# The second 1024 columns of the gates and projections computed with tokens stationary

## The chip, the cores and the metric

The kernel runs on one core of a Trainium2 chip. The metric is the device time of one execution in microseconds, the median of several runs.

## The reference

One decoder block over 256 tokens of width 2048, all in fp32. From the condition vector `c` six vectors of 2048 are made with the matrix `w_ada` (they scale, shift and gate). Then:

```
proj = h @ w_in                       # h: normed, scaled, shifted x
u, q, k, v, ga, gb = split(proj)      # 1024, 1024, 1024, 1024, 2048, 2048 columns
y_ssm = s5_branch(u)                  # state-space scan, gelu, times sigmoid(y @ w_glu + b)
y_att = moba_attention(q, k, v)
merged = sigmoid(ga) * (y_ssm @ w_proj_ssm) + sigmoid(gb) * (y_att @ w_proj_attn)
x = x + g1 * (merged @ w_out)
x = x + g2 * (square(relu(h2 @ w_ff1)) @ w_ff2)
return rms_norm(x, g)
```

## The kernel before

**Matmuls in three pieces.** Each fp32 operand is split in two fp32r parts, a rounded `hi` and the rest `lo`, and a product is hi*hi + hi*lo + lo*hi. For weights this is done as they stream in (`stream`, `split`): SP issues a load of 128 rows by 1024 columns, 512 KB, into one of 7 `wraw` buffers (L153), ScalarE casts `whi` (L158), VectorE subtracts to `wlo` (L160), each in 4 buffers. Such a k tile of 1024 columns is called a unit here.

**Two forms of a pass.** A pass takes one group of 1024 weight columns through all its k tiles, into four PSUM banks of a ring of five. `gemm_t` (L194 to L196) keeps the weights stationary and streams the 256 tokens: 8 blocks of 128 columns, three matmuls of 256 columns each, 24 a unit; the result lies with weight columns on the partitions and tokens along the row. `gemm_n` (L235 to L237) keeps 128 tokens stationary and streams 512 weight columns: 2 token halves, 2 column halves, three matmuls each, 12 a unit; the result has tokens on the partitions. `w_out` and `w_ff2` and the values of attention use `gemm_n`; q, k, u, the gates and the projections use `gemm_t`.

**The order of work around the change.** After q, k, v, u and the first half of `ga` come three passes over `w_in` of 16 units each: the second half of `ga` (5120), `gb` first half (6144) and second half (7168). Then, of 8 units each: proj_attn columns 0 to 1023, w_glu, proj_attn columns 1024 to 2047, proj_ssm in two passes; then w_out in two passes of 16 units. The attention runs between the matmuls of the first gate pass, the scan from its ninth unit on through the other two.

**Lanes.** Side jobs sit in lanes. After each unit `step` adds the lane's rate to its credit and starts a job for each whole credit. The lane `ada` holds the sums for `w_ada`: a job loads 512 KB into a `wraw` buffer (L289) and has VectorE multiply and sum an earlier one (L296). Its rate is set by stage: R4 for the last 12 units of k and v, RS0 for the first 8 units of the second `ga` pass, RS1 from there, RS2 in the last gate pass, RS3 in proj_attn 0, RPA from w_glu to proj_ssm, RWO in w_out. The lane `m` holds attention at rate RAT, then 14 scan jobs at rate RSS: for each of four blocks the inputs, the scan and the outputs, then gelu and `hop_out`, which turns the result around by 32 small DMAs on POOL's queue into `yT`. Within this, the order on each engine is fixed at build time by the framework's scheduler, from priorities and its own estimate of times.

**From the scan to the merge.** `yT` holds tokens as (s c), s being the position within four. It is split into `yy` (`split` called with `sc4`), the input of w_glu; its sigmoid `sg` is multiplied by `yT` (L1201) and split into `gg`, the input of proj_ssm. All these keep the (s c) order of tokens. `gb` is multiplied by the proj_attn banks (L1181). The merge then, bank by bank, multiplies `ga` by the proj_ssm bank and restores the order of tokens on the way by a view with stride four on `ga` (L1212), adds `gb` (L1213) and splits the sum into `mh`, `ml`, the stationary operands of w_out.

Of the kernel before, what the change touches and what calls it, by code (L numbers as in the profile page):

```python
# [19 lines left out]
P = 128  # L20
S = 256
D = 2048
KT = D // P
# [24 lines left out]
R1 = .92  # L48
R2 = .56
R3 = .0  # L50
R4 = .5
RS0 = .6
RS1 = .3
RS2 = .3
RS3 = .7
GR = (4, 6, 6)
RAT = 1.5
RSS = .43
RPA = .88
RWO = .6  # L60
RM = 1.05
# [15 lines left out]
class Kern:  # L77
# [136 lines left out]
                                               stop=i == n - 1 and k == 1, skip_group_check=True)  # L214
        return banks

    def gemm_n(self, src, kts, c0, xh, xl, koff=0, tail=1):
        nc = self.nc
        banks = self.four("pn")
        n = len(kts)  # L220
        held, prev = [], None
        for i, unit in enumerate(self.stream(src, kts, c0)):
            u = (i,) + unit
            held.append(u)
            for t in range(2):
                if t and n - tail <= i < n - 1:
                    continue
                tk = slice(t * P, (t + 1) * P)
                for s in range(2):
                    o = banks[t * 2 + s]  # L230
                    c = slice(s * 512, (s + 1) * 512)
                    for q, kt, hi, lo in held if t else [u]:
                        kx = kt - koff
                        with self.after(prev if tail > 1 and i == n - 1 and t + s else None):
                            nc.tensor.matmul(o, xh[:, kx, tk], hi[:, c], start=q == 0, stop=False)  # L235
                            nc.tensor.matmul(o, xl[:, kx, tk], hi[:, c], start=False, stop=False)  # L236
                            self.mm = last = nc.tensor.matmul(o, xh[:, kx, tk], lo[:, c], start=False, stop=q == n - 1)  # L237
                    prev = last
                if t:
                    held = []  # L240
        return banks
# [658 lines left out]
    def body(self):  # L900
        nc, a, v = self.nc, self.a, self.nc.vector
# [62 lines left out]
        win = a["w_in"][0]  # L964
# [130 lines left out]
        nop = lambda: None  # L1095
# [26 lines left out]
        self.flush("ssm")  # L1122
        self.lanes["ada"][1] = R4
        self.bias_load()
        qkvu(1, 2, 2)
        qkvu(2, 2, 2)
        ga = self.ga
        self.asc = ga[:, 8:14, :].rearrange("p k s -> p (k s)").rearrange("p (i n) -> p i n", i=2)
        self.yatt = self.slot("S5", [P, 8, S], name="yatt")
        gb = self.slot("S1", [P, KT, S], name="gb")  # L1130
        tabs = {}

        def start():
# [14 lines left out]
        self.lane("m", self.attn_jobs() + [start], RAT, 1.0)  # L1148
        self.lanes["ada"][1] = RS0

        def to_ssm():
            self.flush("m")
            self.lane("m", bgl, RSS)
            self.lanes["ada"][1] = RS1

        for i in range(1, 4):
            if i == 3:
                self.lanes["ada"][1] = RS2
            dst, c0 = ((ga, 4096), (ga, 5120), (gb, 6144), (gb, 7168))[i]
            banks = self.gemm_t(win, range(KT), c0, self.ah, self.al, mid={8: to_ssm} if i == 1 else {})  # L1160
            for b in range(4):
                nc.scalar.copy(dst[:, (i % 2) * 8 + 2 * b:(i % 2) * 8 + 2 * b + 2, :],
                               banks[b].rearrange("p (k s) -> p k s", s=S))
        self.flush("m")
        self.lanes["ada"][1] = RS3

# [6 lines left out]
        yh = self.slot("SV", [P, 8, S], F32R, name="yh")  # L1173
        yl = self.slot("T", [P, 8, S], F32R, name="yl")
        for k in range(4):
            self.split(yh[:, 2 * k:2 * k + 2], yl[:, 2 * k:2 * k + 2], self.yatt[:, 2 * k:2 * k + 2])
        def proj_attn(cg):
            banks = self.gemm_t(a["w_proj_attn"][0], range(8), cg * 1024, yh, yl)
            for b in range(4):
                d = gb[:, cg * 8 + 2 * b:cg * 8 + 2 * b + 2, :].rearrange("p k s -> p (k s)")  # L1180
                v.tensor_mul(d, d, banks[b])  # L1181

        proj_attn(0)
        self.lanes["ada"][1] = RPA
        yy = self.slot("VT", [P, 2, 8, S], F32R, name="yy")
        yT = self.yT.rearrange("p s k c -> p k s c")
        sc4 = lambda z: z.rearrange("p k (s c) -> p k s c", s=4)
        self.gate, self.hgate = self.done[-4]
        for k in range(4):
            self.split(sc4(yy[:, 0, 2 * k:2 * k + 2]), sc4(yy[:, 1, 2 * k:2 * k + 2]), yT[:, 2 * k:2 * k + 2])  # L1190
# [1 line left out]
        banks = self.gemm_t(a["w_glu"][0], range(8), 0, yy[:, 0], yy[:, 1])  # L1192
        gg = self.slot("QT", [P, 2, 8, S], F32R, name="gg")
        sg = self.slot("S5", [P, 4, 2, S], name="sg")
        for b in range(4):
            t = sg[:, b]
# [3 lines left out]
            s = slice(2 * b, 2 * b + 2)  # L1200
            v.tensor_mul(sc4(t), sc4(t), yT[:, s])  # L1201
            self.split(gg[:, 0, s], gg[:, 1, s], t)
        proj_attn(1)
        m2 = self.slot("A2", [P, 2, KT, S], F32R, name="mh")
        mh, ml = m2[:, 0], m2[:, 1]
        for cg in range(2):
            banks = self.gemm_t(a["w_proj_ssm"][0], range(8), cg * 1024, gg[:, 0], gg[:, 1])
            for b in range(4):
                s = slice(cg * 8 + 2 * b, cg * 8 + 2 * b + 2)
                d = ga[:, s, :]  # L1210
                dk = d.rearrange("p k (c s) -> p k s c", s=4)
                v.tensor_mul(dk, dk, banks[b].rearrange("p (k s c) -> p k s c", k=2, s=4))  # L1212
                v.tensor_add(d, d, gb[:, s, :])  # L1213
                self.split(mh[:, s], ml[:, s], d)
        self.lane("x", self.load_x(), .25, -.5)
        self.lane("g1", [lambda ch=ch: g1_row(ch) for ch in range(4)], .25)
        self.lanes["ada"][1] = RWO
# [3 lines left out]
        for cg in range(2):  # L1221
# [6 lines left out]
            banks = self.gemm_n(a["w_out"][0], range(KT), cg * 1024, mh, ml, tail=TW if cg else 1)  # L1228
# [3 lines left out]
            with self.hot():  # L1232
                for b in range(4):
                    t, c = b // 2, slice(cg * 1024 + (b % 2) * 512, cg * 1024 + (b % 2) * 512 + 512)
# [141 lines left out]
        for g in range(NP):  # L1376
            part = self.slot(("S4", "T", "SV", "S5")[g], [P, 4, 512], name="part")
            if g:
                banks = self.gemm_t(w1, range(0, 8), g * 1024, self.ah, self.al)
            else:  # L1380
                wh, wl = [self.slot(n, [P, 4, 1024], F32R, name="wf") for n in ("VT", "QT")]
                banks = self.gemm_t(w1, range(0, 4), 0, hp[:, 0], hp[:, 1], mid={2: h_first, 3: h_second},
                                    homes=[(wh[:, k, :], wl[:, k, :]) for k in range(4)])
# [79 lines left out]
```

## Time and profile before

| | |
|---|---|
| median of 3 runs | 1403.18 us (1402.85 to 1406.64) |
| the profiled execution | 1404.23 us, of which the span is 1402.5 us |
| TensorE matmul busy | 1374.0 us, 9704 matmuls |
| VectorE busy | 1062.9 us |
| ScalarE busy | 702.7 us |
| DMA | 356.61 MB, 254 GB/s over the span |

PE is TensorE, PEld its weight loads, DVE VectorE, ACT ScalarE, SP the engine that issues the weights' DMAs, POOL GpSimd. A group's row names the line, the engine, the operation, what is written and read, the shapes, the count, busy microseconds and mean nanoseconds of one, and after a bar the idle time just before them with what ended it. A windows row gives, for a stretch of the span, its length, then busy microseconds and instruction count of PE, PEld, DVE, ACT and POOL, the granted clock of TensorE, the busy share of the DMA engines and GB/s. A timeline row starts with the start and the duration in microseconds.

### The profile page before, as it was taken

What the parts mean: (1) busy time and instruction counts of PE and PEld (TensorE: products, weight loads), DVE (VectorE), ACT (ScalarE), POOL (GpSimd) and SP (SyncE); (2) the same over time, 40 slices, a digit from 0 to 9 for tenths busy, and PEclk for the clock granted to TensorE, in tenths of its full rate; (3) what the DMA queues carried; (4) which work ended last, traced back from release to release, by engine and by line L of the source; (5) the groups of instructions that cost most, each with busy time, mean ns of one, the idle gap of its engine ahead of it and who ended that gap; (6) DMA issues with size and microseconds to landing.
All of it is one profiled execution on the core that took longest, in us unless ns stands there. A gap on an engine that the chain in (4) does not pass through costs nothing.

```text
span 1402.5 us, 24287 instructions
## 1 busy us (share of the span) xinstructions
PE 1374.0 (98%) x9704; PEld 1240.5 (88%) x9704; DVE 1062.9 (76%) x1480; ACT 702.7 (50%) x926; POOL 42.5 (3%) x95
## 2 busy tenths in 40 slices
PE   6999999999999999999999999999999999999996
PEld 5899999999999999888999888888888888888885
DVE  5699998786997888979896976767666455555676
ACT  4554444357446743445546654544453553635534
POOL 1000000400004000000000000000000000000000
PEclk9999999999999999999999999999999999999998
DMA  9999864785558889899698878797878666566561
GB/s 373 383 401 339 326 235 139 243 276 164 174 184 252 294 302 341 290 356 323 215 372 288 303 248 249 250 252 281 249 235 246 194 192 191 186 194 185 183 202 61
DMA packets 112434, 356.61 MB, mean 254 GB/s; under 512 B 12240, under 2 KB 12272, under 8 KB 111904
## 3 DMA queue, kind: packets, MB, share of 16 engines
q1 hardware_dynamic: 109424, 349.23, 73.3%
q0 software_dynamic: 2896, 5.83, 1.4%
q8 instruction: 76, 1.25, 0.4%
q14 instruction: 38, 0.31, 0.1%
HBM read 350.79 MB, written 2.51 MB: 252 GB/s over the span
## 4 chain that ended last, share of the span: by engine, by line
PE 92%; DVE 3%; ACT 1%; DMA 1%; issue 1%; SPq 0%; DVEq 0%; ACTq 0%
PE pd L211 13%; PE pn L235 11%; PE pn L237 11%; PE pn L236 11%; PE pt L194 11%; PE pt L196 11%; PE pt L195 11%; PE pd L213 7%; DVE wlo L160 1%; PE trv L664 1%; PE ys L882 1%; PE rk L698 1%; ACT whi L158 1%; PE adap L266 1%; DVE wraw L296 0%
## 5 line engine op out<-in xcount | busy, mean ns | idle before, releaser
L158 ACT CAST whi<-wraw 128x1024 fp32r<-128x1024 f32 x452 | 473.6, 1051 | 574.8 <-PE pn L236 174.0
L160 DVE TENSOR_TENSOR wlo<-wraw,whi 128x1024 fp32r<-128x1024 f32 x452 | 550.2, 1221 | 264.9 <-ACT whi L158 261.7
L211 PE MATMUL pd<-h2h,whi 128*128 128x512 f32 x800 | 281.7, 397 | 0.0
L194 PE MATMUL pt<-ah,whi 128*128 128x256 f32 x896 | 251.5, 287 | 5.4 <-ACT ah L158 5.1
L195 PE MATMUL pt<-ah,whi 128*128 128x256 f32 x896 | 252.7, 285 | 0.0
L196 PE MATMUL pt<-ah,wlo 128*128 128x256 f32 x896 | 246.3, 285 | 1.7 <-DVE wlo L160 1.7
L213 PE MATMUL pd<-h2h,wlo 128*128 128x256 f32 x800 | 224.2, 281 | 0.0
L235 PE MATMUL pn<-whi,ff 128*128 128x512 f32 x512 | 199.3, 389 | 0.0
L236 PE MATMUL pn<-whi,ff 128*128 128x512 f32 x512 | 199.2, 389 | 0.0
L237 PE MATMUL pn<-wlo,ff 128*128 128x512 f32 x512 | 198.0, 389 | 0.0
L211 PEld LDWEIGHTS pd<-h2h,whi 128*128 128x128 f32 x800 | 150.1, 188 | 36.3
L194 PEld LDWEIGHTS pt<-ah,whi 128*128 128x128 f32 x896 | 170.9, 193 | 7.9 <-ACT ah L158 6.0
L195 PEld LDWEIGHTS pt<-ah,whi 128*128 128x128 f32 x896 | 172.4, 192 | 1.5 <-issue 0.8
L196 PEld LDWEIGHTS pt<-ah,wlo 128*128 128x128 f32 x896 | 168.7, 192 | 2.4 <-DVE wlo L160 2.1
L296 DVE SCALAR_TENSOR_TENSOR wraw<-wraw,cb 128x1024 f32<-128x1024 f32 x128 | 155.7, 1217 | 0.0
L213 PEld LDWEIGHTS pd<-h2h,wlo 128*128 128x128 f32 x800 | 151.1, 189 | 0.4
L237 PEld LDWEIGHTS pn<-wlo,ff 128*128 128x128 f32 x512 | 96.1, 188 | 20.2
L235 PEld LDWEIGHTS pn<-whi,ff 128*128 128x128 f32 x512 | 96.1, 188 | 20.0
L236 PEld LDWEIGHTS pn<-whi,ff 128*128 128x128 f32 x512 | 96.1, 188 | 19.7
L338 DVE SCALAR_TENSOR_TENSOR ahm<-ahm,cb 128x2048 f32<-128x2048 f32 x24 | 54.8, 2281 | 0.0
L194 PE MATMUL pt<-h2h,whi 128*128 128x256 f32 x192 | 52.6, 286 | 0.8 <-ACT whi L158 0.5
L235 PE MATMUL pn<-whi,mh 128*128 128x512 f32 x128 | 50.2, 392 | 2.1 <-ACT whi L158 2.1
(371 smaller groups left out, 1839.9 us busy)
## 6 DMA issues: line engine op xcount, KB each, us to landing
wraw<-in_w_ff_dram SPq DMA_DIRECT2D x256, 512.0 KB, 4.7
wraw<-in_w_in_dram SPq DMA_DIRECT2D x128, 512.0 KB, 5.5
wraw<-in_wat_dram SPq DMA_DIRECT2D x128, 512.0 KB, 5.8
ahm<-in_wat_dram SPq DMA_DIRECT2D x48, 512.0 KB, 6.9
wraw<-in_w_out_dram SPq DMA_DIRECT2D x32, 512.0 KB, 6.4
wraw<-in_w_proj_attn_dram SPq DMA_DIRECT2D x16, 512.0 KB, 5.5
wraw<-in_w_proj_ssm_dram SPq DMA_DIRECT2D x16, 512.0 KB, 6.2
ahm<-in_wan_dram SPq DMA_DIRECT2D x8, 512.0 KB, 11.2
```

The costliest lines, as they stand in the source:

```text
L158: h = self.nc.scalar.copy(hi, src)
L160: s = self.nc.vector.tensor_sub(lo, src, hi.bitcast(F32))
L194: nc.tensor.matmul(o, hi[:, c], xh[:, kx, :], start=st, stop=False, skip_group_check=True)
L195: nc.tensor.matmul(o, hi[:, c], xl[:, kx, :], start=False, stop=False, skip_group_check=True)
L196: self.mm = nc.tensor.matmul(o, lo[:, c], xh[:, kx, :], start=False, stop=sp, skip_group_check=True)
L211: nc.tensor.matmul(banks[blk], hi[:, c], x2[:, :, kt, :], start=i + k == 0, stop=False, skip_group_check=True)
L213: self.mm = nc.tensor.matmul(banks[blk][:, S:2 * S], lo[:, c], x2[:, 0, kt, :], start=False, stop=i == n - 1 and k == 1, skip_group_check= ...
L235: nc.tensor.matmul(o, xh[:, kx, tk], hi[:, c], start=q == 0, stop=False)
L236: nc.tensor.matmul(o, xl[:, kx, tk], hi[:, c], start=False, stop=False)
L237: self.mm = last = nc.tensor.matmul(o, xh[:, kx, tk], lo[:, c], start=False, stop=q == n - 1)
L296: v.scalar_tensor_tensor(w, w, 1.0, self.cb[:, (i % 2) * 1024:(i % 2 + 1) * 1024], op0=OP.mult, op1=OP.mult, accum_out=pc[:, i:i + 1])
L338: v.scalar_tensor_tensor(w, w, 1.0, self.cb, op0=OP.mult, op1=OP.mult, accum_out=pc[:, i:i + 1])
```

## The change

The passes over the second 1024 columns of `ga`, `gb`, proj_attn and proj_ssm become `gemm_n`, so these halves (`ga2`, `gb2`, views of the same buffers) hold tokens on the partitions. `yy` and `sg` are written in the natural order of tokens (a view with stride four), since token blocks are now stationary in proj_ssm; the merge needs no reordering any more. The second half of the merge multiplies and adds token-major; four jobs of a new lane, `turned`, one after each of the fourth to seventh units of w_out's first pass, transpose two column tiles each on TensorE into a PSUM bank of the other ring (three banks) and split from there into `mh`, `ml`. The rates R4, RS0, RS1, RS2 and RSS change. `gemm_n` learns `mid`, a job at a given unit.

```diff
-R4 = .5
-RS0 = .6
-RS1 = .3
-RS2 = .3
+R4 = .7
+RS0 = .8
+RS1 = .2
+RS2 = .2
-RSS = .43
+RSS = .4
...
+        ga2, gb2 = [z[:, 8:16, :].rearrange("p k s -> p (k s)").rearrange("p (t c) -> p t c", t=2) for z in (ga, gb)]
...
-            dst, c0 = ((ga, 4096), (ga, 5120), (gb, 6144), (gb, 7168))[i]
-            banks = self.gemm_t(win, range(KT), c0, self.ah, self.al, mid={8: to_ssm} if i == 1 else {})
+            c0 = 4096 + 1024 * i
+            if i == 2:
+                banks = self.gemm_t(win, range(KT), c0, self.ah, self.al)
+                for b in range(4):
+                    nc.scalar.copy(gb[:, 2 * b:2 * b + 2, :], banks[b].rearrange("p (k s) -> p k s", s=S))
+                continue
+            banks = self.gemm_n(win, range(KT), c0, self.ah, self.al, mid={8: to_ssm} if i == 1 else {})
             for b in range(4):
-                nc.scalar.copy(dst[:, (i % 2) * 8 + 2 * b:(i % 2) * 8 + 2 * b + 2, :],
-                               banks[b].rearrange("p (k s) -> p k s", s=S))
+                nc.scalar.copy((ga2 if i == 1 else gb2)[:, b // 2, (b % 2) * 512:(b % 2) * 512 + 512], banks[b])
...
-            banks = self.gemm_t(a["w_proj_attn"][0], range(8), cg * 1024, yh, yl)
+            banks = (self.gemm_n if cg else self.gemm_t)(a["w_proj_attn"][0], range(8), cg * 1024, yh, yl)
...
-        sc4 = lambda z: z.rearrange("p k (s c) -> p k s c", s=4)
+        sc4 = lambda z: z.rearrange("p k (c s) -> p k s c", s=4)
...
+        def turned(k0):
+            p = self.aux("trm")
+            for i in range(4):
+                with self.after(self.mm):
+                    c = (k0 - 8 + i // 2) * P
+                    nc.tensor.transpose(p[:, i * P:(i + 1) * P], gb2[:, i % 2, c:c + P], self.ident)
+            self.gate, self.hgate = self.done[-1]
+            self.split(mh[:, k0:k0 + 2], ml[:, k0:k0 + 2], p.rearrange("p (k s) -> p k s", s=S))
+            self.gate = self.hgate = None
+
+        banks = self.gemm_t(a["w_proj_ssm"][0], range(8), 0, gg[:, 0], gg[:, 1])
...
+            v.tensor_mul(df, df, banks[b])
+            v.tensor_add(d, d, gb[:, s, :])
+            self.split(mh[:, s], ml[:, s], d)
+        banks = self.gemm_n(a["w_proj_ssm"][0], range(8), 1024, gg[:, 0], gg[:, 1])
+        for b in (0, 2, 1, 3):
+            c = slice((b % 2) * 512, (b % 2) * 512 + 512)
+            d, e = ga2[:, b // 2, c], gb2[:, b // 2, c]
+            v.tensor_mul(d, d, banks[b])
+            v.tensor_add(e, e, d)
+        self.lane("turn", [nop] * 3 + [lambda k0=k0: turned(k0) for k0 in range(8, 16, 2)], 1.0)
```

More of the change, by code (lines that the diff above doesn't have):

```diff
@@ L215, in gemm_d, with gemm_n @@
         return banks
-    def gemm_n(self, src, kts, c0, xh, xl, koff=0, tail=1):
+    def gemm_n(self, src, kts, c0, xh, xl, koff=0, tail=1, mid={}):
         nc = self.nc
@@ L224, in gemm_n @@
             held.append(u)
+            if i in mid:
+                mid[i]()
             for t in range(2):
@@ L1177, in proj_attn @@
         def proj_attn(cg):
-            banks = self.gemm_t(a["w_proj_attn"][0], range(8), cg * 1024, yh, yl)
+            banks = (self.gemm_n if cg else self.gemm_t)(a["w_proj_attn"][0], range(8), cg * 1024, yh, yl)
             for b in range(4):
-                d = gb[:, cg * 8 + 2 * b:cg * 8 + 2 * b + 2, :].rearrange("p k s -> p (k s)")
+                d = gb[:, 2 * b:2 * b + 2, :].rearrange("p k s -> p (k s)")
+                if cg:
+                    d = gb2[:, b // 2, (b % 2) * 512:(b % 2) * 512 + 512]
                 v.tensor_mul(d, d, banks[b])
@@ L1205, in body @@
         mh, ml = m2[:, 0], m2[:, 1]
[L1206 to L1214, printed above, removed]
+        def turned(k0):
[8 more added lines that the diff above has]
+        banks = self.gemm_t(a["w_proj_ssm"][0], range(8), 0, gg[:, 0], gg[:, 1])
+        for b in range(4):
+            s = slice(2 * b, 2 * b + 2)
+            d = ga[:, s, :]
+            df = d.rearrange("p k s -> p (k s)")
+            v.tensor_mul(df, df, banks[b])
[8 more added lines that the diff above has]
+        self.lane("turn", [nop] * 3 + [lambda k0=k0: turned(k0) for k0 in range(8, 16, 2)], 1.0)
         self.lane("x", self.load_x(), .25, -.5)
```

## The prediction

> **What bounds the kernel now.** I read the page first, then PE's waits, then a table of stages by windows, then the timeline of single matmuls.
>
> ```profile
> span 1402.5 us, 24287 instructions
> PE 1374.0 (98%) x9704; PEld 1240.5 (88%) x9704; DVE 1062.9 (76%) x1480; ACT 702.7 (50%) x926; POOL 42.5 (3%) x95
> PE   6999999999999999999999999999999999999996
> PEclk9999999999999999999999999999999999999998
> ```
> ```profile
> PE ss L446 <- DVE junk L444: 7.1, 1, 7.1
> PE pt L194 <- ACT ah L158: 5.1, 5, 3.2
> PE pn L235 <- ACT whi L158: 2.1, 1, 2.1
> ```
>
> TensorE is busy for 98% of the span at full clock. Its two longest waits lie in the first slice, where the first columns are prepared; the third, 2.1 us, lies where w_out begins. So the time is TensorE's own work, and a microsecond taken from that work comes off the end, unless a wait takes its place.
>
> The stages that the change touches, in order: the second gate pass (292.43 to 349.97, attention between its matmuls), the third (to 412.10, the scan), the fourth (to 464.45, the scan's end), proj_attn 0, w_glu, proj_attn 1, the two passes of proj_ssm (533.78 to 585.98), then w_out.
>
> ```profile
> core 0: us, PE busy (x) PEld busy (x) DVE busy (x) ACT busy (x) POOL busy (x), PEclk, DMA share, GB/s
> 292.43:349.97 57.54, 57.54 (x464) 56.74 (x462) 41.74 (x76) 39.79 (x83) 0.00 (x0) 1.00 0.64 219
> 349.97:412.10 62.13, 62.13 (x838) 60.68 (x837) 61.14 (x84) 28.99 (x38) 0.00 (x0) 1.00 0.55 177
> 412.10:464.45 52.35, 52.35 (x579) 51.95 (x577) 39.96 (x50) 34.08 (x43) 15.30 (x32) 1.00 0.77 241
> 464.45:487.49 23.04, 23.04 (x195) 23.04 (x193) 19.29 (x28) 16.34 (x20) 0.00 (x0) 1.00 0.84 296
> 487.49:510.74 23.25, 23.25 (x196) 23.25 (x195) 18.03 (x26) 7.93 (x8) 0.00 (x0) 1.00 0.91 328
> 510.74:533.78 23.04, 23.04 (x194) 23.04 (x193) 20.49 (x30) 12.52 (x20) 0.00 (x0) 1.00 0.85 298
> 533.78:558.39 24.61, 24.40 (x205) 24.21 (x203) 22.68 (x32) 9.82 (x10) 0.00 (x0) 1.00 0.96 345
> 558.39:585.98 27.59, 25.53 (x211) 25.20 (x210) 26.44 (x36) 12.13 (x16) 0.00 (x0) 1.00 0.84 299
> 597.34:627.26 29.92, 29.92 (x133) 24.77 (x132) 22.73 (x30) 11.12 (x12) 0.00 (x0) 1.00 0.94 357
> 644.27:649.71 5.44, 5.44 (x26) 4.50 (x24) 3.61 (x5) 5.13 (x9) 0.00 (x0) 1.00 0.94 325
> 649.71:652.88 3.17, 3.17 (x17) 2.65 (x16) 3.17 (x5) 1.31 (x2) 0.00 (x0) 1.00 0.82 300
> ```
>
> PE fills every window up to 533.78; in the next two it idles 0.21 and 2.06 us. VectorE is full in the scan (61.14 of 62.13) and nearly so in the last two projection windows.
>
> **The gain: four passes change form.** Where the stage has nothing else on TensorE, units are exactly periodic:
>
> ```profile
> 479.93 0.28 PE L194 MATMUL pt<-yh,whi 128*128 128x256 f32 x1
> ...
> 482.81 0.28 PE L194 MATMUL pt<-yh,whi 128*128 128x256 f32 x1
> ```
> ```profile
> 597.34 0.39 PE L235 MATMUL pn<-whi,mh 128*128 128x512 f32 x1
> ...
> 600.06 0.39 PE L235 MATMUL pn<-whi,mh 128*128 128x512 f32 x1
> ```
>
> A gemm_t unit has 24 matmuls of 256 columns: one k tile takes 482.81 - 479.93 = 2.88 us, 120.0 ns a matmul. A gemm_n unit has 12 of 512 columns for the same products: 2.72 us, 226.7 ns each. (The 0.28 and 0.39 us are latencies that overlap; the distance of starts is the cost.) The windows agree: eight units in 23.04 us, eleven in 29.92. The change turns 16 + 16 + 8 + 8 = 48 units, so it removes 48 x 0.16 = **7.7 us** of TensorE's path. Both attention and scan matmuls lie between the units of the first two passes, in number unchanged. Half as many weight loads remain, and in the 597.34 window they are less busy (24.77 of 29.92) than in the gemm_t windows.
>
> The Trainium skill, "TensorE: Matmul & The Clock Gate", section "Wait — 56ns, not 53.3ns?", gives a start-to-start of N / 2.4 GHz plus about 2.5 ns. By it a unit would lose only 12 x 2.5 = 30 ns, and 48 units 1.4 us. The rows differ: 120.0 ns at 256 columns and 226.7 at 512 leave 13.3 ns a matmul, so the measured 0.16 is used.
>
> **The cost on TensorE: 16 transposes.** The token-major second half of the merge must return to columns; four groups of four 128x128 transposes go behind the fourth to the seventh unit of w_out. Groups of four like these exist in w_out's second pass:
>
> ```profile
> 651.98 0.60 PE L734 MATMUL trh<-ident,x 128*128 128x128 f32 x4
> ```
>
> The unit with them took 3.17 us; the two before it 5.44, 2.72 each. So a group costs 0.45 us, four **1.8 us**. From below it is 4 x 0.36 (the next matmul starts 0.36 us after the first transpose) = 1.4; the whole unit's excess is the nearer row, since it holds the switch back. The Trainium skill, same page, section "Part 4: PE-mode transpose", has about 275 ns for one in a kernel's context; by that 16 cost 4.4 us and the sum below would end at 1400.4. The trace shows 272 ns as latency and not as spacing, so it stays out.
>
> **VectorE and ScalarE: strides moved.**
>
> ```profile
> L160 DVE TENSOR_TENSOR wlo<-wraw,whi 128x1024 fp32r<-128x1024 f32 x452 | 550.2, 1221 | 264.9 <-ACT whi L158 261.7 <-PE pt L196 1.5 <-PE pn L237 0.8
> L296 DVE SCALAR_TENSOR_TENSOR wraw<-wraw,cb 128x1024 f32<-128x1024 f32 x128 | 155.7, 1217 | 0.0
> L1212 DVE TENSOR_TENSOR ga<-ga,pt 128x512 f32<-128x512 f32 x8 | 8.5, 1094 | 0.0
> L1213 DVE TENSOR_TENSOR ga<-ga,gb 128x512 f32<-128x512 f32 x8 | 5.3, 679 | 0.0
> L160 DVE TENSOR_TENSOR mh<-ga,mh 128x512 fp32r<-128x512 f32 x8 | 5.3, 678 | 0.0
> L1201 DVE TENSOR_TENSOR sg<-sg,yT 128x512 f32<-128x512 f32 x4 | 2.5, 682 | 0.0
> L160 DVE TENSOR_TENSOR yy<-yT,yy 128x512 fp32r<-128x512 f32 x4 | 2.5, 680 | 0.0
> ```
>
> The merge's multiply reads and writes SBUF four elements apart: 1094 ns against 679 for its contiguous neighbour. With tokens in order it becomes contiguous: 8 x 0.415 = 3.3 us less. The same stride goes to the four yy splits and the four sg multiplies (680 and 682 now): 8 x 0.415 = 3.3 us more, 1.65 in proj_attn 0 (19.29 of 23.04 busy, room) and 1.65 in proj_attn 1 (20.49 of 23.04, little room). ScalarE's four yy casts write strided too, which no row shows: between nothing and the same factor, 1094/679, on
>
> ```profile
> 470.52 2.17 ACT L158 CAST yy<-yT 128x512 fp32r<-128x512 f32 x4
> 449.74 0.96 POOL L803 DMA_DIRECT2D yT<-u  x2 [0.31 <-DMA yT<-u]
> ```
>
> which is 1.3 us more; I take the upper end, free, since w_glu first needs yy at 487.49. The four split pairs of the merge's second half leave proj_ssm for w_out's first pass (4 x 0.68 on VectorE, where 22.73 of 29.92 are used in the 597.34 window).
>
> **The respacing.** Sums per unit, 12 units of R4, 8 of RS0, 8 + 16 of RS1, 16 of RS2: before 6 + 4.8 + 7.2 + 4.8 = 22.8, after 8.4 + 6.4 + 4.8 + 3.2 = 22.8. So from the projections on the same sums are due, each with its 512 KB load on SP's queue. In the third gate pass 1.6 sums of 1.3 us leave a full VectorE; that saves no time, as PE has no gap there. The early ones go where DMA has 0.64 of its time used. At .4 the scan's 14 jobs end after 35 steps and not 33, two units, 5.8 us later, and with them the 32 hop DMAs on POOL's queue, which holds nothing else there; the last of them was issued by 450.7 and its reader ran at 470.5, so w_glu does not see it. Cost nothing; were the cover gone, each unit of delay would cost 2.8 us.
>
> **The one wait.** It ends with w_out's first weights:
>
> ```profile
> 572.30 6.66 DMA wraw<-in_w_out_dram
> 579.07 1.05 ACT whi L158
> ```
>
> The load could only be issued when VectorE freed a buffer at 572.3. From 510.74 to 585.98 VectorE is busy 69.61 of 75.24 us. After the change it has 1.65 more (sg) and 4 x 0.415 less (merge) there, so still 69.6, and TensorE wants the stretch in 75.24 - 2.27 - 2.56 = 70.4 us: it would be 99% full. In proj_attn 1 it has 23.04 - 20.49 = 2.55 us free; sg and the faster pass use up 1.65 + 8 x 0.16 = 2.9. The order 0, 2, 1, 3 of the new merge holds a bank back as well: w_out's first unit wants its third bank, freed by the multiply of bank 1, 1.4 us after the pass ends; bank 0 is complete 2.0 us before that end, and two pairs and the third multiply take 5 x 0.68 = 3.4 us, so the multiply ends just then, and later by 1.2 us if a weight split comes between. For both together I estimate 0.5 us more waiting; bounds are the 2.06 us gone and the 2.56 us of these two passes not gained.
>
> **The sum.** -7.7 + 1.8 + 0.5 = -5.4 us. The profiled execution took 1404.23 (span 1402.5), 1.05 over the median 1403.18; applied to the median: **1397.8 us**, 0.38% faster. A measurement of this kernel tells about 0.3%, 4.2 us, from no change.
>
> **Rivals.**
> *The wait goes.* The merge's first half loses its strides, so the buffer is free sooner: -7.7 + 1.8 - 2.1 = -8.0, 1395.2. For it: VectorE's work just ahead of 572.3, the merge's first half, falls by 1.65. Against: sg adds as much in the pass before. Chance 0.14.
> *VectorE becomes the bound from 510.74 on.* The 99% above; proj_attn 1 and proj_ssm 1 gain nothing, and the wait grows by 1: -5.1 + 1.8 + 1.0 = -2.3, 1400.9. Against: VectorE ran 61.14 of 62.13 in the scan with no PE gap. Chance 0.18.
> *The form gains nothing there.* If the 120.0 ns are a property of those stages and not of the 256 columns (the skill's rule above says so in effect, -1.4), then 0 to -1.4 plus 1.8: 1403.6 to 1405. Against: w_out and both gemm_t stages run on the same clock, 1.00. Chance 0.08.
> *The transposes wait (slower).* They stand in PE's in-order queue, with w_out's units behind them, and need the 8 multiplies and adds of the merge, 5.4 us of VectorE. If those get only what splits and sums leave, 2.72 - 1.22 - 0.6 x 1.3 = 0.72 us a unit, they take 7.6 units, 20.5 us, and if they start 9 us late they end 30 us after w_out starts; the last group is due after seven units, 19. PE waits 11: -5.9 + 11 = +5.1, 1408.3. It decides when the last add ends over 29 us after w_out's start. Against:
>
> ```profile
> L1213 DVE TENSOR_TENSOR ga<-ga,gb x8: 671/676/687, 562.0 to 594.3; 128x512 f32<-128x512 f32 x8
> ```
>
> the last add ended at 595, 9 us after the last proj_ssm unit at 585.98, with strides and splits still among them. Chance 0.08.
>
> **The numbers.** The forecast's chance is 0.52, with 1396 to 1399.6 of its own. The range 1394.3 to 1402.6 takes in the first two rivals and leaves out the last two, 0.16, and a little of each tail. Faster by over 0.3% means under 1399.0: 0.44 of the forecast and the 0.14, 0.58; slower, over 1407.4: 0.10 with a remainder for mishaps; within: 0.32.
>
> **What would show it.** Units at 2.72 us in the four passes wherever nothing lies between them; 3.17 us for the four w_out units with transposes; L1212's multiply at 680 ns, sg and the yy difference near 1094; one PE wait of 2 to 3 us at w_out's first weights. It is wrong if these passes keep 2.88, if PE's idle time from 510 us to w_out's end grows by over 2 us, or if transposes wait for the adds.

## The result and the profile after

The changed kernel takes 1410.63 us (median of 4 runs, 1408.9 to 1412.5) where the kernel before took 1404.45 beside it: a ratio of 1.0053 (95% interval 1.0039 to 1.0068). It is slower by half a per cent, 12.8 us above the forecast and outside the forecast's range. The profiled execution took 1410.49 us, its span is 1408.7, 6.2 more than before. The page hides the loss:

```profile
span 1408.7 us, 23174 instructions
PE 1373.7 (98%) x9144; PEld 1213.9 (86%) x9144; DVE 1063.0 (75%) x1480; ACT 703.7 (50%) x926; POOL 42.5 (3%) x95
PE   6999999999899999999999999999999999999996
```

TensorE runs 560 matmuls fewer and is busy just as long as before (1373.7 against 1374.0 us). So a part of the loss lies in time that counts as busy. One slice of forty, the eleventh, shows an 8. Four rows of TensorE's waits tell more (columns: total, times, longest; L237 is L235 of the kernel before). Before they held 1.7, 1.1, 2.1 and 0 us:

```profile
PE pt L196 <- DVE wlo L160: 6.1, 4, 3.7
PE pt L194 <- ACT whi L158: 2.4, 4, 1.0
PE pn L237 <- ACT whi L158: 1.6, 4, 0.7
PE pn L239 <- DVE wlo L160: 1.1, 2, 0.6
```

The table of stages says where. From the second gate pass to the end of w_out's own matmuls:

```profile
292.93:347.66 54.73, 54.47 (x262) 45.04 (x261) 41.20 (x73) 31.90 (x68) 0.00 (x0) 1.00 0.74 253
347.66:415.53 67.87, 64.13 (x844) 62.68 (x843) 59.99 (x81) 36.54 (x53) 0.00 (x0) 0.97 0.46 143
415.53:465.42 49.89, 49.89 (x386) 41.64 (x385) 39.03 (x48) 33.60 (x43) 15.28 (x32) 1.00 0.72 227
465.42:488.46 23.04, 23.04 (x194) 23.03 (x193) 20.09 (x27) 18.07 (x20) 0.00 (x0) 1.00 0.79 268
488.46:511.50 23.04, 23.04 (x195) 23.04 (x194) 18.96 (x27) 8.40 (x9) 0.00 (x0) 1.00 0.96 363
511.50:533.28 21.78, 21.78 (x98) 18.03 (x97) 21.47 (x29) 11.22 (x19) 0.00 (x0) 1.00 0.81 282
533.28:560.85 27.57, 25.30 (x193) 24.68 (x192) 21.53 (x30) 9.33 (x9) 0.00 (x0) 0.94 0.96 340
560.85:583.08 22.23, 21.51 (x94) 17.12 (x93) 22.23 (x32) 9.35 (x11) 0.00 (x0) 1.00 0.79 264
583.08:679.80 96.72, 94.99 (x445) 78.21 (x443) 80.33 (x109) 48.21 (x61) 0.00 (x0) 1.00 0.91 330
```

| stage | before | after | forecast of the change | measured |
|---|---|---|---|---|
| second gate pass | 57.54 | 54.73 | -2.56 | -2.81 |
| third gate pass | 62.13 | 67.87 | 0 | **+5.74** |
| fourth gate pass | 52.35 | 49.89 | -2.56 | -2.46 |
| proj_attn 0 and w_glu | 46.29 | 46.08 | 0 | -0.21 |
| proj_attn 1 | 23.04 | 21.78 | -1.28 | -1.26 |
| proj_ssm to the end of w_out | 139.75 | 146.52 | +1.0 | **+6.77** |

(The last row goes from the first matmul of proj_ssm to the last three of w_out, 533.78 to 673.53 before; its forecast is -1.28 + 1.8 + 0.5.) What the change does to the passes came as forecast. The loss lies in two places that the forecast held still. Both windows have a granted clock under 1.00, which no window from 292 to 653 us had before.

**First place, the third gate pass.** VectorE's timeline:

```profile
348.89 1.23 DVE L160 TENSOR_TENSOR wlo<-wraw,whi 128x1024 fp32r<-128x1024 f32 x1 [0.39 <-ACT whi L158]
351.92 0.69 DVE L829 TENSOR_TENSOR tbl<-tbl 128x512 f32<-128x512 f32 x1 [1.80 <-ACT tbl L828]
353.28 0.69 DVE L829 TENSOR_TENSOR tbl<-tbl 128x512 f32<-128x512 f32 x1 [0.67 <-ACT tbl L828]
358.30 0.69 DVE L848 TENSOR_TENSOR rw<-cone,mag 128x512 f32<-128x512 f32 x1 [4.33 <-PE pav L781]
...
367.85 0.68 DVE L848 TENSOR_TENSOR rw<-cone,mag 128x512 f32<-128x512 f32 x1
368.45 1.22 DVE L160 TENSOR_TENSOR wlo<-wraw,whi 128x1024 fp32r<-128x1024 f32 x1
```

No weight split lies between 348.89 and 368.45. In that gap VectorE first stands idle: the scan's first block begins with L848, which writes `rw`, a tile in the buffer of attention's values, and so waits 4.33 us for the last matmul of attention (`pav`). Then 14 instructions of the scan run in one piece. The idle time itself held no split back, since a split needs ScalarE's cast, and the next casts came only after it:

```profile
362.54 3.89 ACT L158 CAST whi<-wraw 128x1024 fp32r<-128x1024 f32 x4 [2.82 <-PE pt L195]
```

They waited for a matmul of the unit in progress, and ahead of that TensorE had 128 matmuls of the scan in one piece, from 358.12 to 362.00. The first of these casts ended at 363.59; its split then stood another 4.9 us behind the scan in VectorE's order. Before, attention had ended earlier among the units, the wait was 0.35 us, 11 matmuls of a unit stood between the scan's first 64 and the next 64, and two splits stood inside the block:

```profile
351.25 0.69 DVE L846 TENSOR_TENSOR rw<-cone,mag 128x512 f32<-128x512 f32 x1 [0.35 <-PE pav L779]
...
352.95 1.21 DVE L160 TENSOR_TENSOR wlo<-wraw,whi 128x1024 fp32r<-128x1024 f32 x1
...
361.35 1.21 DVE L160 TENSOR_TENSOR wlo<-wraw,whi 128x1024 fp32r<-128x1024 f32 x1
```

TensorE runs out of split weights, and when it starts again it is slow (its timeline, then windows of the changed kernel):

```profile
365.70 0.28 PE L195 MATMUL pt<-ah,whi 128*128 128x256 f32 x1
369.72 0.39 PE L196 MATMUL pt<-ah,wlo 128*128 128x256 f32 x1 [3.74 <-DVE wlo L160]
```
```profile
366.00:370.00 4.00, 0.28 (x2) 0.28 (x3) 4.00 (x6) 0.43 (x1) 0.00 (x0) 1.00 0.00 0
370.00:374.00 4.00, 4.00 (x24) 3.66 (x24) 4.00 (x5) 1.05 (x1) 0.00 (x0) 0.57 0.68 171
```

A pause of 3.74 us, then four microseconds at a mean clock of 0.57, which count as busy and cost 4 x 0.43 = 1.7 us: 5.4 of the 5.74. (Seven of attention's matmuls also moved from the second pass into this one.) The Trainium skill, "TensorE: Matmul & The Clock Gate", section "What's actually happening", states that an idle window of about 3.4 us takes the clock to half, and about as long a busy one back. This pause and the slow stretch behind it, 3.41 us at a clock of 0.50 from 370.42 on, agree.

**Second place, around proj_ssm.** The chain of waits from 525 to 540 us holds these pieces:

```profile
529.46 7.01 DMA wraw<-in_w_proj_ssm_dram
...
536.57 1.05 ACT whi L158
```

The load was issued only at 529.46, when VectorE freed a buffer (in proj_attn 1 it is busy 21.47 of 21.78 us); it landed 7.01 us later. TensorE pauses three times within four microseconds, for 0.52, 0.76 and 0.99 us, and then its clock falls:

```profile
537.00:538.00 1.00, 0.33 (x1) 0.33 (x2) 1.00 (x4) 0.62 (x1) 0.00 (x0) 0.84 1.04 426
538.00:539.00 1.00, 1.00 (x6) 1.00 (x6) 1.00 (x2) 0.00 (x0) 0.00 (x0) 0.50 1.01 414
...
541.00:542.00 1.00, 1.00 (x10) 1.00 (x9) 1.00 (x4) 0.00 (x0) 0.00 (x0) 0.96 1.07 324
```

This proj_ssm pass takes 27.57 us, where e9 below shows 23.21 without the pauses: 4.4 us. Over the whole row, TensorE is without a matmul for 4.72 us where it was for 2.27 before (at w_out's first weights 1.73 now, 2.06 before), the slow clock takes 1.7, and -1.28 with the 2.0 us of the transposes (below) adds 0.7: 4.9 of the 6.77. The rest was not followed up. A part is that a pause costs more than its idle time: a matmul counts as busy for 0.28 us while in an unbroken row the next starts 0.12 us after it, so 0.16 us a pause, by an estimate 0.8 us for five pauses more than before.

### The profile page after: what moved, and what is told of

Its sections match the earlier page's. It is cut to its first block, busy times and chain, and to the rows that moved or that the text cites. A ratio compares the mean times of both kernels' runs of the same rounds, so it can differ in the third digit from the quotient of the medians.

```text
span 1408.7 us, 23174 instructions
## 1 busy us (share of the span) xinstructions
PE 1373.7 (98%) x9144; PEld 1213.9 (86%) x9144; DVE 1063.0 (75%) x1480; ACT 703.7 (50%) x926; POOL 42.5 (3%) x95
## 4 chain that ended last, share of the span: by engine, by line
PE 89%; DVE 5%; DMA 3%; ACT 2%; issue 1%; DVEq 0%; SPq 0%; ACTq 0%
PE pn L237 13%; PE pn L238 13%; PE pn L239 13%; PE pd L211 13%; PE pt L194 8%; PE pt L196 8%; PE pt L195 8%; PE pd L213 7%; DVE wlo L160 2%; DVE wraw L298 1%; ACT whi L158 1%; PE trv L666 1%; PE ys L884 1%; PE rk L700 1%; PE adap L268 1%
## 5 line engine op out<-in xcount | busy, mean ns | idle before, releaser
L237 PE MATMUL pn<-whi,ff 128*128 128x512 f32 x512 | 199.3, 389 | 0.0
L194 PE MATMUL pt<-ah,whi 128*128 128x256 f32 x640 | 178.8, 289 | 5.4 <-ACT ah L158 5.1
L195 PE MATMUL pt<-ah,whi 128*128 128x256 f32 x640 | 179.8, 286 | 0.0
L196 PE MATMUL pt<-ah,wlo 128*128 128x256 f32 x640 | 172.4, 286 | 5.4 <-DVE wlo L160 5.4
L194 PEld LDWEIGHTS pt<-ah,whi 128*128 128x128 f32 x640 | 122.4, 194 | 7.7 <-ACT ah L158 6.0
L195 PEld LDWEIGHTS pt<-ah,whi 128*128 128x128 f32 x640 | 123.9, 194 | 1.5 <-issue 0.8
L196 PEld LDWEIGHTS pt<-ah,wlo 128*128 128x128 f32 x640 | 119.8, 194 | 6.2 <-DVE wlo L160 6.0
L237 PEld LDWEIGHTS pn<-whi,ff 128*128 128x128 f32 x512 | 96.1, 188 | 20.0
L237 PE MATMUL pn<-whi,ah 128*128 128x512 f32 x192 | 75.9, 397 | 0.3 <-ACT whi L158 0.3
L238 PE MATMUL pn<-whi,ah 128*128 128x512 f32 x192 | 75.2, 392 | 0.0
L239 PE MATMUL pn<-wlo,ah 128*128 128x512 f32 x192 | 70.8, 394 | 0.0
```

Source lines behind the costliest of these rows:

```text
L194: nc.tensor.matmul(o, hi[:, c], xh[:, kx, :], start=st, stop=False, skip_group_check=True)
L195: nc.tensor.matmul(o, hi[:, c], xl[:, kx, :], start=False, stop=False, skip_group_check=True)
L196: self.mm = nc.tensor.matmul(o, lo[:, c], xh[:, kx, :], start=False, stop=sp, skip_group_check=True)
```

## The experiments

Theory A: the loss is two stalls that the new forms make, by VectorE's fixed order in the third gate pass and by a full VectorE ahead of proj_ssm. Theory B: the respaced sums and scan jobs make it. All times are medians beside the kernel before on the same chip.

**e1 and e2: each half alone.** e1 is the kernel before with the five new rates; e2 the changed kernel with the five old ones. (The five lines are written as one here; e2 has the opposite edit.)

```diff
-R4, RS0, RS1, RS2, RSS = .5, .6, .3, .3, .43
+R4, RS0, RS1, RS2, RSS = .7, .8, .2, .2, .4
```

> The kernel before with the five new rates alone. Theory A (order): the loss comes from VectorE's fixed order, in which a whole scan block stands ahead of the next weight split while attention ends late, and from the load chain ahead of proj_ssm; it needs the faster passes, so rates alone give no stall in the third gate pass (62 to 63 us) and a total within 2 us of before, 1402.5 to 1406.5. Theory B (respacing): the new rates are the loss, 5 us in the third gate pass, so 1409 to 1411 here.

> The changed kernel with the old five rates. Theory A: in this kernel's order on VectorE a split stands inside the first scan block, so the third gate pass takes 62 to 64 us and not 67.9; the wait at the first proj_ssm pass stays (27 us and not 24.6): 1400 to 1405. Theory B: without the new rates both stalls go, 1398 to 1400.

e1: 1404.71 against 1402.14, 1.0016 (1.0007 to 1.0025). e2: 1411.12, 1.0061 (1.0046 to 1.0076). The third gate pass in e1, then in e2:

```profile
351.36:413.49 62.13, 62.13 (x838) 60.69 (x837) 59.41 (x80) 30.19 (x41) 0.00 (x0) 1.00 0.57 179
```
```profile
344.10:413.69 69.59, 65.62 (x855) 63.56 (x854) 60.40 (x87) 38.03 (x57) 0.00 (x0) 1.00 0.47 151
```

Theory B falls: the rates alone cost 0.16% and make no stall. The forms alone cost all of it. But A failed on e2 too: it had this pass at 62 to 64 us and the total at 1400 to 1405, and the pass got longer (69.59 against 67.87). Its 4.0 us without a matmul are not for split weights either: there TensorE waits for the scan's own results (`ys` for `sri`, 3.0 us in three waits, `vi` for `rw`, 0.9), at full clock. So the forms bring a stall with either set of rates, but which one depends on the rates.

**e3 and e8: the scan later.** The scan's lane starts with idle steps, so that its jobs come later among the units.

```diff
-        bgl = []
+        bgl = [nop, nop]   # e3;  e8: [nop], and RSS = .43
```

> The changed kernel with two empty jobs ahead of the scan's 14, so each scan job comes five units later. Theory A: the first scan block has splits between its steps again and attention is over when it starts; the third gate pass falls from 67.9 us to 62 to 64, total 1404.5 to 1407. If the stall does not come from the order of scan and splits, the pass stays at 67 to 68 and the total at 1410.

> The changed kernel with one empty job ahead of the scan's and RSS at .43, so that the first scan blocks come some two units later and hop_out at the same unit as now. In VectorE's order splits then stand between the steps of the first block. Theory A: the third gate pass falls from 67.9 to 60 to 63 us, w_glu does not wait for yy: total 1405 to 1407. If instead the whole scan only moves, the fourth pass gets longer by as much and the total stays at 1410.

e3: 1411.79, 1.0069 (1.0052 to 1.0087), 4.8 us above the expected range. The third pass falls to 58.41 us, but 160 of the scan's matmuls moved into the fourth, which rises to 56.14; the two together take 114.55 us for 117.76 in the changed kernel, and no pause is left in them. But the cover that the prediction named is gone: the scan ends later, and two waits of TensorE for the first operand of w_glu appear:

```profile
PE pt L195 <- DVE yy L160: 3.0, 1, 3.0
PE pt L194 <- ACT yy L158: 2.5, 1, 2.5
```

e8, one step with the old scan rate: 1407.67, 1.0019 (1.0008 to 1.003), 0.7 us above its range. The third pass is at 63.82 us, at full clock, and nothing waits for yy; proj_ssm's first pass still takes 29.05 us.

```profile
346.84:410.66 63.82, 62.92 (x845) 61.47 (x843) 56.00 (x76) 38.27 (x55) 0.00 (x0) 1.00 0.48 150
```

In both, attention ends as late as in the changed kernel, and VectorE's wait of 4.33 us for it is still there. What is new is that splits stand inside the block behind it, as in these rows of e9 (below), which has e8's lane:

```profile
357.90 0.69 DVE L848 TENSOR_TENSOR rw<-cone,mag 128x512 f32<-128x512 f32 x1 [4.33 <-PE pav L781]
...
361.52 1.22 DVE L160 TENSOR_TENSOR wlo<-wraw,whi 128x1024 fp32r<-128x1024 f32 x1
```

On TensorE, too, matmuls of a unit again stand behind the first 64 of the scan (9 in e8, 23 in e3). So the stall comes from the block that stands in one piece, and not from the wait ahead of it. How much of it is VectorE's order and how much TensorE's, no run separates.

**e4: the second gate pass in its old form.** If the new form of that pass is what sets attention late among the units, the stall goes with it.

```diff
-            banks = self.gemm_n(win, range(KT), c0, self.ah, self.al, mid={8: to_ssm} if i == 1 else {})
+            banks = (self.gemm_t if i == 1 else self.gemm_n)(win, range(KT), c0, self.ah, self.al, mid=...)
```

> The changed kernel with the second ga pass as gemm_t again (its output put down untransposed, so the merged values of those 1024 columns are not the reference's). Theory A: the pass takes 2.3 us more, the third gate pass 62 to 64 and not 67.9: total 1406 to 1408. Theory B: the third gate pass stays at 67 to 68 since the rates are the new ones, total 1412 to 1413.

1407.43, 1.0035 (1.002 to 1.0049). The third pass:

```profile
349.62:411.75 62.13, 62.13 (x838) 60.69 (x837) 59.40 (x80) 30.19 (x41) 0.00 (x0) 1.00 0.58 178
```

62.13 us again, as before the change, and attention's last product starts 1.0 us into this pass, where it starts 10.2 us into it in the changed kernel and 0.9 before. The 2.8 us won in one pass bring 5.74 us of loss in the next, whose own form was never touched.

**e5, e6 and e7: what fills VectorE ahead of proj_ssm.** Three suspects, one each: the faster proj_attn 1 (e5), the strides of yy and sg (e6), the sums for w_ada (e7).

```diff
-            banks = (self.gemm_n if cg else self.gemm_t)(a["w_proj_attn"][0], range(8), cg * 1024, yh, yl)
+            banks = self.gemm_t(a["w_proj_attn"][0], range(8), cg * 1024, yh, yl)   # e5
-        sc4 = lambda z: z.rearrange("p k (c s) -> p k s c", s=4)
+        sc4 = lambda z: z.rearrange("p k (s c) -> p k s c", s=4)                    # e6
-RPA = .88
+RPA = .7                                                                            # e7
```

> The changed kernel with proj_attn's second pass as gemm_t again (its output meets gb2 untransposed, so those merged columns are not the reference's). If the wait at the first proj_ssm pass comes from the faster pass ahead of it, that pass falls from 27.6 us to 24 to 25 while proj_attn 1 goes from 21.8 to 23.0: total 1408 to 1409. If it comes from the strided multiplies alone it stays at 27 or more and the total goes to 1411 to 1412. The third gate pass stays near 67.9 in both.

> The changed kernel with yy and sg in the old order of tokens (the merge then pairs the wrong tokens in proj_ssm's part, so the output is not the reference's). The sg multiplies go back from 1100 to 680 ns, 1.7 us of VectorE ahead of proj_ssm. If these strides carry the wait there, the pass falls from 27.6 to 25 to 26 us, total 1408 to 1409; if not, 27 to 28 and 1410 to 1411.

> The changed kernel with RPA at .7 for .88: six sums fewer, 7.8 us of VectorE and 3 MB of DMA, from w_glu to proj_ssm. If VectorE and the loads that wait on it bound this stretch (the second rival), the wait at the first proj_ssm pass goes (23 to 24.5 us for 27.6) and the one at w_out shrinks: total 1405 to 1407, unless the sums left over cost it back in w_out. If the wait has another cause: no change, 1410.

e5: 1409.12, 1.0038 (1.0026 to 1.005), where 1411 to 1412 was expected with the pass unchanged. e6: 1407.68, 1.0031 (1.002 to 1.0043). e7: 1406.70, 1.0024 (1.0013 to 1.0034). proj_ssm's first pass in e5, e6 and e7:

```profile
533.48:560.65 27.17, 24.87 (x195) 24.64 (x194) 22.31 (x32) 8.19 (x8) 0.00 (x0) 0.94 0.91 332
```
```profile
531.94:556.82 24.88, 23.28 (x193) 23.08 (x192) 22.24 (x32) 9.45 (x9) 0.00 (x0) 1.00 0.98 367
```
```profile
533.73:558.20 24.47, 23.30 (x193) 23.09 (x192) 19.03 (x27) 9.45 (x9) 0.00 (x0) 1.00 0.94 357
```

The faster pass is not the cause (27.17 of 27.57 us stay, and the clock is 0.94 again). Without the strides, or with fewer sums, the pass takes 24.9 or 24.5 us at full clock, with one pause of 1.60 or 1.17 us left. What both take away is VectorE's work ahead of it. e6 leaves every load as it was, so DMA traffic alone is not the cause; but it also halves ScalarE's `yy` casts, and e7 also drops six loads, so VectorE as the cause is what the two have in common and was not changed by itself. (e6 meets the slow clock later instead, at w_out from 583.21 on.)

**e9 and e12: both mended, and a control.** e9 joins e8 and e7; e12 is the kernel before with e7's rate, since that rate may help by itself.

> The changed kernel with the scan one job later (RSS .43) and RPA at .7. Theory A, two separate stalls: the gains of the two runs add, third gate pass 61 to 64 us, first proj_ssm pass 23.5 to 24.7: total 1402 to 1404.5. If the second stall only moves (as it grew to 29 us in the run with the later scan), the total stays at 1406 to 1408.

> The kernel before with RPA at .7, a control: it has one wait of 2 us at w_out's first weights. If a lower rate helps any kernel here, that wait shrinks: 1400.5 to 1402 where before is 1402.5. If it matters only where the passes are faster: no change within 1 us.

e9: 1400.09 against 1403.02, 0.9978 (0.9968 to 0.9987), 0.2% faster than before and 2 us better than expected. e12: 1403.08, 0.9996 (0.9987 to 1.0005), no change. The third gate pass and proj_ssm's first pass of e9:

```profile
347.27:410.20 62.93, 62.93 (x844) 61.52 (x842) 55.11 (x75) 38.26 (x55) 0.00 (x0) 1.00 0.49 152
528.06:551.27 23.21, 23.21 (x193) 23.08 (x192) 19.56 (x27) 9.45 (x9) 0.00 (x0) 1.00 0.94 356
```

No time without a matmul is left in either. Between e9 and e12, which share the rate of the sums there, the change with its later scan is worth 1400.09 - 1403.08 = -3.0 us, of the -5.9 that passes and transposes should give. Some 3 us still go in proj_ssm and w_out, where e9 needs 140.68 us and e12 137.18 and the forms alone would add 0.5. In part this is a wait at w_out's first weights (1.4 and 0.5 us in e9, none over 0.5 in e12 there); the rest stays open. And e7's rate only defers sums: in e12 the wait of 2.06 us at w_out's first weights is gone, but the stretch behind w_out takes 717.6 us, and 716.5 in e9, for 714.7 before.

**e10 and e11: the strides made cheaper, the sums held back.** Both start from e9. In e10 the sigmoid reads PSUM in turned order and writes the natural one, so that only the read of `yT` in sg's multiply is strided (512 elements from one to the next), and yy keeps the old order. e11 adds a low rate for the sums in proj_ssm.

```diff
-        sc4 = lambda z: z.rearrange("p k (c s) -> p k s c", s=4)
+        sc4 = lambda z: z.rearrange("p k (s c) -> p k s c", s=4)
...
-                nc.scalar.activation(t[:, k], banks[b][:, k * S:(k + 1) * S], AF.Sigmoid,
+                nc.scalar.activation(t[:, k].rearrange("p (c s) -> p c s", s=4),
+                                     banks[b][:, k * S:(k + 1) * S].rearrange("p (s c) -> p c s", s=4), AF.Sigmoid,
...
-            v.tensor_mul(sc4(t), sc4(t), yT[:, s])
+            tn = t.rearrange("p k (c s) -> p k c s", s=4)
+            v.tensor_mul(tn, tn, yT[:, s].rearrange("p k s c -> p k c s"))
...
+        self.lanes["ada"][1] = .4     # e11 alone, ahead of proj_ssm's first pass
```

> As the run before, and the order of tokens is restored by the sigmoid's read of PSUM instead of by the yy splits; only yT is read with a stride, in the four sg multiplies. If a strided SBUF read alone costs as much as read and write together, sg stays at 1100 ns and yy falls from 1125 (VectorE) and 1163 (ScalarE) to 680 and 545; if the write is what costs, sg falls to 680 as well. Less VectorE ahead of proj_ssm: first proj_ssm pass 23.1 to 23.8 us, total 1400 to 1403.

> As the run before, with the sums' rate at .4 in the two proj_ssm passes. If the wait at w_out's first weights comes from VectorE freeing buffers late, w_out (96.5 us from its first matmul to its last, with 93.3 of work) falls to 94 to 95 and the total to 1398.5 to 1401; if the sums held back cost it later, w_out stays and the total is 1401 to 1404.

e10: 1401.2, 0.9991 (0.9982 to 1.0); no gain over e9. Its sg multiply is as slow as in the changed kernel (1100 ns):

```profile
L1212 DVE TENSOR_TENSOR sg<-sg,yT 128x512 f32<-128x512 f32 x4 | 4.3, 1110 | 0.0
```

e11: 1407.59, 1.0027 (1.0016 to 1.0038), above both expected ranges. It reaches the first matmul of the stage behind w_out 6.25 us earlier than the kernel before (681.58 for 687.83), and then pays for the sums held back, in one wait of TensorE that is 1.2 us long in e9, e10 and e12, and in 6.83 us at a clock of 0.50 behind it:

```profile
PE pd L211 <- ACT whi L158: 6.8, 1, 6.8
```

## Why the prediction was wrong

**The gain was right.** In the fourth gate pass the units, now in the form `gemm_n`, start 2.72 us apart:

```profile
449.10 0.39 PE L237 MATMUL pn<-whi,ah 128*128 128x512 f32 x1
...
451.82 0.39 PE L237 MATMUL pn<-whi,ah 128*128 128x512 f32 x1
```

The passes gave 2.81 (with seven of attention's matmuls gone to the next pass) + 2.46 + 1.26 us of the forecast 2.56 + 2.56 + 1.28. So the third rival (no gain from the form) falls, and with it the Trainium skill's start-to-start rule as a price here.

**The transposes were right.** A unit with four takes 3.22 us, 0.50 more than without, 2.0 in all against 1.8. None waited for an add, so the fourth rival falls.

```profile
602.71 0.40 PE L237 MATMUL pn<-whi,mh 128*128 128x512 f32 x1
...
604.79 0.60 PE L1221 MATMUL trm<-ident,gb 128*128 128x128 f32 x4
...
605.93 0.40 PE L237 MATMUL pn<-whi,mh 128*128 128x512 f32 x1
```

**The strides were right on VectorE, too low on ScalarE.** The merge's multiply fell from 1094 to 680 ns, sg and yy rose to 1100 and 1125. ScalarE's four yy casts went from 2.17 us to 4.0, a factor of 1.9 where I had bounded it by 1.6; it was hidden.

```profile
L160 DVE TENSOR_TENSOR yy<-yT,yy 128x512 fp32r<-128x512 f32 x4 | 4.2, 1125 | 0.0
L1210 DVE TENSOR_TENSOR sg<-sg,yT 128x512 f32<-128x512 f32 x4 | 4.2, 1100 | 0.0
L158 ACT CAST yy<-yT 128x512 fp32r<-128x512 f32 x4 | 4.0, 1163 | 0.0
```

**The step that failed first** is the third gate pass, which the sum -7.7 + 1.8 + 0.5 puts at nothing. The only sentence on it is "1.6 sums of 1.3 us leave a full VectorE; that saves no time, as PE has no gap there". I took it as a stage of its own that keeps its 62.13 us, because its form does not change; it took 67.87. The gap that PE lacked before came with the change. Attention's steps stand between the units' matmuls in TensorE's order: from a head's transposes to its product 25 to 36 matmuls of `gemm_t` before, 3.0 to 4.3 us, and in four of the eight heads now 22 of `gemm_n`, 5.1 us. So the second gate pass got shorter by 2.8 us and attention got longer, 65.0 us from the start of that pass to its last product for 58.5, and its end moved from 350.9 to 357.9 us. Behind it the scan's first block stands in one piece. e4 takes away the late end, and the stall goes; e3 and e8 keep the late end and put units' work inside the block, and the stall goes as well. Why the fixed order has the block in one piece there, the runs do not show. I had asked what stands behind a waiting instruction for the transposes on TensorE, and not for the scan's block.

**The second step that failed** is "For both together I estimate 0.5 us more waiting", with the 2.56 us of proj_attn 1 and proj_ssm 1 as upper bound. The mechanism stands in part in the prediction as the second rival: VectorE full from 510.74 on. It was full in proj_attn 1 (21.47 of 21.78 us), which still gained its 1.26 us; over the three passes it was busy for 65.2 of 71.6 us, and not 99%, as it had to wait for late loads itself. The rival's price was too small, 2.6 us of lost gain and 1.0 of wait, where some 6 were lost: I had charged a late split only with its own lateness. A late split frees its buffer late, the next load is issued late (529.46) and takes 7.01 us to land, and the pauses that follow lower the clock for another 1.7 us. No sentence of the prediction reckoned with the clock, which stood at 1.00 in every windows row that I had read. That e6 and e7, and not e5, mend this pass says that the strides' time counted and the 1.28 us of the faster pass did not. One sign of being wrong that the prediction names was seen: PE's idle time from 510 us to w_out's end grew by 2.45 us.

**The respacing** was not free: alone it costs 0.16% (e1). With the forms its worth cannot be told (e2 and the changed kernel: 1.0061 and 1.0053, within each other's intervals).

## What to carry to other kernels

In a kernel bound by one engine, a pass that changes its form moves the engines' other work against it: side work that stands between its matmuls can get slower while the pass gets faster. Look in the fixed order of every engine on the operands' way for a block that stands in one piece, and count the operands behind it. Price a starved engine with what follows too: the buffer freed late, the load issued late, the clock. And when a rate is turned down to mend a stall, look where the deferred work is done; e11 lost there all that it had won.

## What the runs showed of the hardware

- The slow clock came in stretches of 3.41 us, or of 6.83, at 0.50, and their starts lie whole stretches apart: 370.42 and 537.67 us in the changed kernel, 167.25 us, which is 49 times 3.413. What tells the falls apart here is the idle time within the stretch of this grid just ahead, and not the length of one pause. In the changed kernel it was 2.7 us ahead of the first, and ahead of the second 2.2, from three pauses of 0.52, 0.76 and 0.99 us, none near the 3.4 us that the Trainium skill names above. The single pause of 2.06 us at w_out's first weights before the change fell on two stretches, 0.37 and 1.69 us, and left the clock at 1.00; so did the pauses of 1.73 us in all there after it, 0.45 and 1.28. In all traces here, from 285 to 770 us, at least 1.4 us of idle time stood ahead of every fall of the clock, and at most 1.7 us where it did not fall; where the limit lies between these is open.
- A read from SBUF in steps of 512 elements, of one input alone, makes a VectorE multiply of 128x512 as slow (1110 ns, e10) as steps of four elements on its output and the other input (1100), against 680 without.
